# A hybrid decoder step on one core: attention steps nearer together, samples after the recurrence, pair closes later

## The chip, the cores and the metric

One core of a Trainium2 chip runs one launch of the program. The metric is the device time of the launch in microseconds (us); lower is better. The engines are TensorE (PE, matmuls and transposes), VectorE (DVE), ScalarE (ACT), GpSimd (POOL) and SyncE (SP), whose queue issues nearly all DMAs of this kernel. Each engine works through its own list of instructions in order, and semaphores hold an instruction back until what it needs is there.

## The reference, cut to what matters

One layer for a prompt of 1024 tokens and for 8 sample sequences with one new token each and caches of past keys and values; width 1024, 24 heads of 64 in three groups of 8.

```python
xn = rms_norm(x, norm_pre)
u, z_rnn, q, k, v, z_attn, g_rnn, g_attn = split(xn @ w_in)          # 1024 x 9216
uc, conv_new = causal_conv(u, conv_buf, conv_w, conv_b)
h, h_last = rg_lru(uc, h0, ...)        # r, i = sigmoid(block-diagonal products), a scan over tokens
y_rnn = (h * silu(z_rnn)) @ w_rnn_out
for g, (window, dilation) in enumerate(((128, 1), (512, 4), (2048, 16))):
    o, lse = dilated_attention(q[g], k[g], v[g], window, dilation, slopes[g])   # ALiBi, softmax
    # the prompt attends within itself; a sample token attends to 129 strided cache rows
y_attn = (merge_dilations(outs, lses) * silu(z_attn)) @ w_attn_out   # softmax over the three lse
mixed = sigmoid(g_rnn) * y_rnn + sigmoid(g_attn) * y_attn
out = x + rms_norm(mixed @ w_out, norm_post)
# also returned: the conv and recurrence states and the new k and v rows
```

## The kernel before

All products are in two-part form: an operand is a high and a low tile (`whi` and `wlo` for weights, written by ACT in line 274 and DVE in line 275), and a product is three matmuls, whi by x high, whi by x low, wlo by x high. Every matmul is recorded at line 183, every transpose by PE at line 187.

The work has these stages. First the norm and eight column blocks of `w_in`. Then the **pair phase**: 16 pairs of column blocks, each by seven products of combined operands (`project_pair`; the combined weights are the `wop` tiles, made by ACT in line 294 and DVE in lines 298 and 301). Products are added up in two tiles, `qa` and `qb` (DVE line 639, ACT line 641). When the fifth product is done, the closing operations of `qa` are put on a list to be emitted later (line 662), and after the seventh those of `qb` (line 666). What they are depends on the pair: a pair "a" takes a sigmoid on ACT (`zo`, line 847), multiplies on POOL (line 850) and stores to `zad` by DMA (line 673); a pair "v" copies to `vo` on ACT (line 829) and stores to `vd`. Beside the pairs runs the first half of the recurrence (`lru_front`, the tiles named `room`).

Then the **attention phase**: for each of four head pairs `hp` and three groups `g`, the projections of k and of q (192 projection matmuls for both, evicted into `kt` by DVE line 1026 and `qt` by ACT line 1022), and the attention of that group, in six steps (`attention`): scores into two PSUM banks, DVE adds the bias and takes the running extremes into `stat` (line 1135), ACT takes the exponential (line 1139), PE transposes `P` (line 1149, `turn`) and multiplies with `vn` (`values`). After a head pair's third group come `merge(hp)`, which weighs the three groups' outputs (`ot`; the weights go through DRAM, `fd` and `fb`), and the sample tokens' attention `sample(hp)`: a transpose of `qn`, a way through DRAM that spreads q over all partitions (`sd`, `qb`), keys from the cache (`ck`) multiplied on POOL and summed on DVE into `sc`, a transpose of `sc`, a softmax in `S`, a transpose of `S`, values from the cache (again `ck`) weighed on POOL (line 1372) and added on DVE (line 1375), and a sum by PE. Beside the first part of attention runs the second half of the recurrence (`lru_back`, lanes "lru" and "lru2", ACT lines 953 to 955 with a table load). Eight late gates follow (`proj_g`, evicted by ACT line 1427 into `sg`), and then the output products.

What sets the order: the program is written by one pass of the builder that keeps an emission clock, `clk`. Each projection matmul that is emitted moves the clock on. Work that is not on the main line stands in **lanes**, queues of generators; a generator yields the clock units after which it wants to be called again, and `tick` calls those that are due. `later` holds functions until the clock has reached their time, first in, first out. So a number such as `STEP` or 2500 is a distance in emitted matmuls, not a time, and the engines then run what stands in their queues as soon as their semaphores allow. Each lane runs one generator at a time: the samples stand in the lane "sample", one behind the other.

Most tiles come from an **arena** of 45 equal slots, whose free list is first in, first out (`Arena.get`). If none is free, the builder forces the clock on (`force`) until one is given back. The two lanes of the recurrence hold rooms of 4 slots each until they end (`lru_end`); a sample waits for 5 free slots (`SPARE`) before it loads. In attention there are three PSUM banks for scores and for all transposes of samples and merges (the tag "s"), used in turn. Before the seventh of the late gates the builder forces the clock until all four merges and samples are done:

```python
        if i == LATE_GATES - 2:
            until(lambda: len(merged) == 4 and len(sampled) == 4)
            spawn("split", split_ya())
```

Of the kernel before, what the change touches and what calls it, by code (L numbers as in the profile page):

```python
# [37 lines left out]

HALF = 520
OPS = 4  # L40
STEP = 3400
SPARE = 5
KY, VY = 3000, 4000
SLOPES = [[2.0 ** (-8.0 * (g * 8 + h + 1) / 24.0) for h in range(8)] for g in range(3)]
# [31 lines left out]
class Room:  # L76
# [15 lines left out]
    def close(self):  # L92
        self.arena.slots.extend(self.slots)
# [3 lines left out]
def hybrid_step(ctx: ExitStack, tc: tile.TileContext, I, O):  # L97
# [18 lines left out]
    def ps_tile(tag, n=1):  # L116
        own = MODES[mode[0]][tag]
        turns[tag] = i = turns.get(tag, -1) + 1
        b = own[i % len(own)]
        return banks[:, b] if n == 1 else banks[:, b:b + n]  # L120
# [4 lines left out]
    waiting, lanes, busy = [], {}, set()  # L125

    def later(delay, fn):
        waiting.append((clk[0] + delay, fn))

    def spawn(lane, gen, delay=0):  # L130
        lanes.setdefault(lane, deque()).append([clk[0] + delay, gen])
# [57 lines left out]
    def advance(gen):  # L189
        for _ in gen:  # L190
            tick()
# [326 lines left out]
    def mm3(out, wh, wl, mh, ml, first, last):  # L518
        mm(out, wh, mh, start=first, stop=False)
        mm(out, wh, ml, start=False, stop=False)  # L520
        mm(out, wl, mh, start=False, stop=last)
# [75 lines left out]
    def x21_back():  # L597
        while len(ar.slots) < 6:
            yield 500
        ts = [new([128, 2, HALF], F32, "xsum") for _ in range(2)]  # L600
        for q, t in enumerate(ts):
            nc.sync.dma_start(t, xd[2 * q:2 * q + 2].rearrange("k p c -> p k c"))
        yield 8000
        for k in range(4):
            x = new([128, 2, HALF], F32R, "x1b")
            src = ts[k // 2][:, k % 2]
            nc.scalar.activation(x[:, 0], src, AF.Copy)
            yield 700
            nc.vector.tensor_tensor(x[:, 1], src, f32(x[:, 0]), op=OP.subtract)
            X[1, k] = x  # L610
        ar.free(*ts)
# [3 lines left out]
    def x_op(name, k):  # L615
        if name[0] == "s":
            return SX[name, k]
        return X[int(name[1]) - 1, k + 4 * (int(name[2]) - 1)]

    def project_pair(close, last=False):  # L620

        i = W.use_pair()
        ta = new([128, 2, HALF], F32, "qa")
        quarter = lambda t, q: t[:, q].rearrange("p (c n) -> p c n", c=2)
        c11, c22 = quarter(ta, 0), quarter(ta, 1)
        for step, (wname, xname) in enumerate(STEPS):
            w = W.op(i, wname)
            if step == 1:
                tb = new([128, 2, HALF], F32, "qb")
                c21, c12 = quarter(tb, 0), quarter(tb, 1)  # L630
            p2 = ps_tile("c", 2)[:, :, :HALF // 2]
            for c in range(2):
                for k in range(4):
                    x = x_op(xname, k)[:, :, HALF // 2 * c:HALF // 2 * (c + 1)]
                    mm3(p2[:, c], w[:, 0, k], w[:, 1, k], x[:, 0], x[:, 1], k == 0, k == 3)
                    if k % 2:
                        W.work()
                        yield None
            add = lambda to, by: nc.vector.tensor_tensor(to, p2, by, op=OP.add)  # L639
            if step == 0:  # L640
                nc.scalar.activation(c11, p2, AF.Copy)
            elif step == 1:
                add(c12, c11)
            elif step == 2:
                add(c21, c12)
            elif step == 3:
                add(c12, c12)
                add(c22, c21)
            elif step == 4:
                add(c11, c11)  # L650
            elif step == 5:
                add(c21, c21)
            else:
                add(c12, c12)
            yield None
            W.drop(i, wname)
            if last and step == 3:
                for k in range(4):
                    ar.free(SX.pop(("s1", k)))
                spawn("sums", x21_back())  # L660
            if step == 4:
                later(2500, lambda: close(((0, 0, ta[:, 0]), (1, 1, ta[:, 1])), ta))
        W.pieces.pop(i)
        W.ops.pop(i)
        W.made.pop(i)
        later(2500, lambda: close(((0, 1, tb[:, 0]), (1, 0, tb[:, 1])), tb))

    def leave(dst, quarters, t, width=NT, then=None):

# [343 lines left out]
    def proj_qkv(g, hp, kind):  # L1013
        t = new([128, SEQ], F32, "qkv"[kind] + "t")
        (qts, kts)[kind][g, hp] = t

        def evac(c0, n, p):
            m = min(n, SEQ - c0)
            dst, src = grouped(t, g, c0, m), tokens(p, g, m)
            sd = smp[:, kind, 4 * g + hp]  # L1020
            if kind == 0:
                nc.scalar.activation(dst, src, AF.Copy, scale=C["qsc"][:, g, hp:hp + 1])
                if m < n:
                    nc.scalar.activation(sd, p[:, m:n], AF.Copy, scale=0.125)
            else:
                nc.vector.tensor_copy(dst, src)
                if m < n:
                    nc.vector.tensor_copy(sd, p[:, m:n])
        yield from project(evac)
# [22 lines left out]
    def load_v(g, hp):  # L1052
        t = vts[g, hp] = new([128, SEQ], F32, "vt")
        nc.sync.dma_start(t, vd[4 * g + hp])
# [49 lines left out]
    def attention(g, hp):  # L1104
# [80 lines left out]
        for i in range(6):  # L1185
# [12 lines left out]
            if i == 5:  # L1198
                ar.free(vns.pop((g, hp)))
                if g == 2:  # L1200
                    spawn("merge", merge(hp), 1000)
            yield STEP

# [322 lines left out]
    for q, (what, i) in enumerate(PAIRS):  # L1526
        advance(project_pair(pair_of(what, i), last=q == len(PAIRS) - 1))
        if q == 1:
            C = late_consts()
# [13 lines left out]

    room["P"] = new([128, 2, 2, 256], F32, "P")
    room["PT"] = [new([128, 2, 4, 128], F32, "PT") for _ in range(2)]
    for hp in range(4):
        for g in range(3):
            load_v(g, hp)
            for kind in (1, 0):
                advance(proj_qkv(g, hp, kind))  # L1550
            spawn("attention", attention(g, hp), 1000)
        spawn("sample", sample(hp), 1000)
# [203 lines left out]
```

## Time and profile before

| | us |
|---|---|
| median of 3 runs (lowest, highest) | 1280.31 (1277.37, 1282.57) |
| the profiled execution's own time | 1278.47 |
| its span | 1276.7 |
| PE busy in the span | 1221.2 (96%) |
| DVE, ACT, POOL busy | 756.2, 599.7, 261.6 |

The profile is of one execution. The busy times of the engines overlap; PE's share of the span says how little of it PE spends waiting. The granted clock that stands beside a stretch is TensorE's, as a share of full speed: 1.00 is 2.4 GHz throughout, and a stretch at less had a part at 1.2 GHz.

### The profile page before, as it was taken

To read this page: it belongs to the slowest core of one execution; us is meant where nothing else is said; L and a number is where in the kernel's file an instruction comes from. 1 tells how busy PE (TensorE), PEld (TensorE's weight loads), DVE (VectorE), ACT (ScalarE), POOL (GpSimd) and SP (SyncE) were. 2 spreads that over 40 slices of the span, in tenths; PEclk is the share of its full clock that TensorE was granted. 3 is DMA by queue.
4 is the path that set the end of the run, shared out by engine and by line. 5 is a ranking of instruction groups with operands and counts; after the bars stand their busy time and mean duration, and the time that the engine had idled before them with its cause. 6 is when DMAs were issued, how large, how long until landed. Compare 5 with 4: busy or idle time off the path is not lost. (4 is left out here: it accounts for less than half of the span.)

```text
span 1276.7 us, 24741 instructions
## 1 busy us (share of the span) xinstructions
PE 1221.2 (96%) x9949; PEld 1176.2 (92%) x9949; DVE 756.2 (59%) x1575; ACT 599.7 (47%) x1271; POOL 261.6 (20%) x280
## 2 busy tenths in 40 slices
PE   8999999999999978999799999899999979999997
PEld 8999999999999978899788989898999979999997
DVE  5558796777686653567477464555444545545226
ACT  7634445646545556756465343343568332222222
POOL 3011042102031201122224505310422210002001
PEclk9999999999999989999899999999999989999999
DMA  8053153436434294354653853651286466313105
GB/s 254 18 174 112 39 186 117 145 113 173 129 112 146 67 257 122 133 176 139 190 161 121 223 154 87 176 139 36 70 231 182 110 240 206 93 55 116 51 18 199
DMA packets 191161, 174.67 MB, mean 137 GB/s; under 512 B 55177, under 2 KB 162665, under 8 KB 191038
## 3 DMA queue, kind: packets, MB, share of 16 engines
q1 hardware_dynamic: 191046, 173.08, 44.5%
q8 instruction: 78, 1.28, 0.4%
q14 instruction: 37, 0.30, 0.1%
HBM read 122.67 MB, written 50.45 MB: 136 GB/s over the span
## 5 line engine op out<-in xcount | busy, mean ns | idle before, releaser
L183 PE MATMUL banks<-x,whi 128*128 128x256 f32 (+1 forms) x2048 | 386.5, 289 | 5.7 <-DVE qb L639 5.7
L183 PEld LDWEIGHTS banks<-x,whi 128*128 128x128 f32 x2048 | 320.1, 192 | 11.9 <-issue 10.6
L183 PE MATMUL banks<-x,wlo 128*128 128x256 f32 (+1 forms) x1024 | 290.6, 284 | 0.2 <-DVE wlo L334 0.2
L183 PE MATMUL banks<-s,wop 128*128 128x260 f32 x1536 | 197.7, 286 | 7.2 <-DVE wop L298 4.3
L183 PEld LDWEIGHTS banks<-s,wop 128*128 128x128 f32 x1536 | 192.1, 191 | 8.6 <-DVE wop L298 5.1
L183 PEld LDWEIGHTS banks<-x,wlo 128*128 128x128 f32 x1024 | 195.6, 191 | 0.4 <-DVE wlo L334 0.4
L275 DVE TENSOR_TENSOR wlo<-wraw,whi 128x512 fp32r<-128x512 f32 x112 | 93.6, 837 | 120.6 <-ACT whi L274 101.0
L183 PE MATMUL banks<-x,wop 128*128 128x260 f32 x1152 | 146.0, 282 | 0.3 <-DVE wop L298 0.2
L183 PEld LDWEIGHTS banks<-x,wop 128*128 128x128 f32 x1152 | 142.0, 188 | 0.7 <-DVE wop L298 0.7
L1139 ACT ACTIVATE P<-P,stat 128x128 f32<-128x128 f32 (+1 forms) x192 | 84.4, 441 | 70.3 <-DVE stat L1135 70.2
L183 PE MATMUL banks<-x1b,whi 128*128 128x264 f32 (+1 forms) x512 | 101.0, 294 | 16.4 <-ACT sg L1427 7.3
L183 PEld LDWEIGHTS banks<-x1b,whi 128*128 128x128 f32 x512 | 82.1, 196 | 18.8 <-ACT sg L1427 7.5
L183 PE MATMUL banks<-wlo,mh 128*128 128x256 f32 (+1 forms) x288 | 78.8, 280 | 0.0
L183 PE MATMUL banks<-x1b,wlo 128*128 128x256 f32 (+1 forms) x256 | 74.4, 290 | 0.0
L274 ACT ACTIVATE whi<-wraw 128x512 fp32r<-128x512 f32 x112 | 68.5, 621 | 12.4 <-DMA wraw<-in_w_in 10.8
L938 ACT ACTIVATE room<-banks,par 64x256 f32<-64x256 f32 (+2 forms) x96 | 52.2, 544 | 46.2 <-PE banks L183 45.0
L183 PE MATMUL banks<-whi,ml 128*128 128x256 f32 x256 | 71.9, 281 | 0.0
L183 PE MATMUL banks<-whi,mh 128*128 128x256 f32 x256 | 71.8, 280 | 0.0
L1135 DVE CUSTOM_DVE_ANT_0 P<-banks,base 128x128 f32<-128x128 f32 (+1 forms) x192 | 56.0, 348 | 17.4 <-PE banks L183 17.3
L294 ACT ACTIVATE wop<-wsum 128x512 fp32r<-128x512 f32 x48 | 30.1, 627 | 72.9 <-DVE wsum L301 59.3
L183 PE MATMUL banks<-hzh,wlo 128*128 128x256 f32 (+2 forms) x192 | 61.3, 319 | 0.0
L183 PE MATMUL banks<-hzl,whi 128*128 128x256 f32 (+2 forms) x192 | 61.3, 319 | 0.0
(280 smaller groups left out, 2270.5 us busy)
## 6 DMA issues: line engine op xcount, KB each, us to landing
wraw<-in_w_in SPq DMA_DIRECT2D x72, 512.0 KB
ck<-in_cache_kv_w SPq DMA_DIRECT2D x24, 512.0 KB
rxd<-room SPq DMA_DIRECT2D x16, 516.0 KB
room<-rxd SPq DMA_DIRECT2D x16, 516.0 KB
sgl<-sgd SPq DMA_DIRECT2D x16, 516.0 KB
xin<-in_x_prompt SPq DMA_DIRECT2D x16, 512.0 KB
vd<-vo SPq DMA_DIRECT2D x24, 256.0 KB
vt<-vd SPq DMA_DIRECT2D x12, 512.0 KB
```

The lines of the kernel that those rows point to most:

```text
L183: nc.tensor.matmul(out, lhsT, rhs, start=start, stop=stop)
L274: nc.scalar.activation(hi[:, a:b], raw[:, a:b], AF.Copy)
L275: nc.vector.tensor_tensor(lo[:, a:b], raw[:, a:b], f32(hi[:, a:b]), op=OP.subtract)
L294: nc.scalar.activation(w[:, 0], src, AF.Copy)
L938: nc.scalar.activation((a, t)[gate][rows, cs], p[at:at + 64, :n], AF.Sigmoid, bias=par[rows, b, 5 + gate:6 + gate])
L1135: nc.vector.tensor_tensor_reduce(out=pt[:, h, :128 * n], in0=ps[h][:, off:off + 128 * n], in1=base, scale=-SLOPES[g][2 * hp + h] * DIL[g], ...
L1139: nc.scalar.activation(pt[:, h, :128 * n], pt[:, h, :128 * n], AF.Exp, scale=-1.0, bias=st[:, g, 0, h, b:b + 1], accum_out=st[:, g, 1, h, ...
```

## The change

Three things change. `STEP`, the distance between two steps of an attention, is 2500 instead of 3400 clock units. The closing operations of a pair are emitted 4000 instead of 2500 units after their product. And a generator `lru_done` stands ahead of the first sample in the lane "sample": it ends when the lane "lru2" of the recurrence is empty, so that no sample is emitted until then. Lines from 1546 on are 5 higher in the changed kernel.

```diff
-STEP = 3400
+STEP = 2500
...
             if step == 4:
-                later(2500, lambda: close(((0, 0, ta[:, 0]), (1, 1, ta[:, 1])), ta))
+                later(4000, lambda: close(((0, 0, ta[:, 0]), (1, 1, ta[:, 1])), ta))
...
-        later(2500, lambda: close(((0, 1, tb[:, 0]), (1, 0, tb[:, 1])), tb))
+        later(4000, lambda: close(((0, 1, tb[:, 0]), (1, 0, tb[:, 1])), tb))
...
     room["PT"] = [new([128, 2, 4, 128], F32, "PT") for _ in range(2)]
+
+    def lru_done():
+        while "lru2" in lanes:
+            yield 1000
+    spawn("sample", lru_done())
     for hp in range(4):
```

The first place is ACT's queue at the close of the first pair "a", whose sigmoid is the row with `zo` (numbers behind a name are the builder's tile numbers). Before:

```order
L294 ACTIVATE wop_4210<-wraw_4045 128x512
L294 ACTIVATE wop_4228<-wsum_4212 128x512
L847 ACTIVATE zo_4238<-qa_4038 128x1040
L294 ACTIVATE wop_4256<-wraw_4045 128x512
L847 ACTIVATE zo_4312<-qb_4078 128x1040
L641 ACTIVATE qa_4281<-banks 128x520
L903 ACTIVATE lh<-lw 128x256
L907 ACTIVATE room_4244<-room_4243,par 128x1056
L294 ACTIVATE wop_4349<-wsum_4212 128x512
L294 ACTIVATE wop_4365<-wraw_4046 128x512
```

The same place now:

```order
L294 ACTIVATE wop_4210<-wraw_4045 128x512
L294 ACTIVATE wop_4228<-wsum_4212 128x512
L294 ACTIVATE wop_4254<-wraw_4045 128x512
L847 ACTIVATE zo_4264<-qa_4038 128x1040
L294 ACTIVATE wop_4286<-wsum_4212 128x512
L641 ACTIVATE qa_4279<-banks 128x520
L294 ACTIVATE wop_4317<-wraw_4046 128x512
L903 ACTIVATE lh<-lw 128x256
L907 ACTIVATE room_4242<-room_4241,par 128x1056
L847 ACTIVATE zo_4331<-qb_4076 128x1040
L294 ACTIVATE wop_4356<-wsum_4212 128x512
L294 ACTIVATE wop_4394<-wraw_4046 128x512
```

Three copies into `wop` (4254, 4286 and 4317) now stand ahead of the operations that they stood behind; before, the copies after `zo_4312` came behind lines 641, 903 and 907.

The second place is ACT's queue at the end of the pair phase, where the last pair "v" closes (`vo`) and the recurrence's first half ends (`room`, lines 907 and 922). Before:

```order
L907 ACTIVATE room_5314<-room_5313,par 128x1056
L274 ACTIVATE whi_5405<-wraw_5291 128x512 x2
L829 ACTIVATE vo_5478<-qa_5274 128x32x16 x2
L922 ACTIVATE room_5482<-room_5315 64x1032
L922 ACTIVATE room_5483<-room_5315 64x1032
L274 ACTIVATE whi_5524<-wraw_5522 128x512
```

Now:

```order
L907 ACTIVATE room_5310<-room_5309,par 128x1056
L294 ACTIVATE wop_5396<-wraw_5108 128x512
L274 ACTIVATE whi_5413<-wraw_5304 128x512 x2
L922 ACTIVATE room_5478<-room_5311 64x1032
L922 ACTIVATE room_5479<-room_5311 64x1032
L829 ACTIVATE vo_5499<-qa_5274 128x32x16 x2
L274 ACTIVATE whi_5524<-wraw_5522 128x512
```

The two copies into `vo` stand behind the recurrence's two operations instead of ahead of them.

The third place is PE's queue between the sixth and the seventh late gate, where the builder waits for all merges and samples (`mw` is merge 3's, `S`, `mn` and the matmuls from `one` are of sample 3, `smp` is for the sample rows). Before:

```order
L183 MATMUL banks<-x_7_32_132,whi_10711 128x264 x2
L183 MATMUL banks<-x_7_32_132,wlo_10712 128x264
L183 MATMUL banks<-one_2065,ck_10689 128x1 x8
L187 MATMUL banks<-ident,mw 48x128
L187 MATMUL banks<-ident,smp 96x128 x2
L183 MATMUL banks<-x_0_17_117,whi_10880 128x256 x2
```

Now:

```order
L183 MATMUL banks<-x_7_32_132,whi_10765 128x264 x2
L183 MATMUL banks<-x_7_32_132,wlo_10766 128x264
L187 MATMUL banks<-ident,S 128x64 x3
L183 MATMUL banks<-mn,e2n 128x24
L183 MATMUL banks<-one_2063,ck_10977 128x1 x8
L183 MATMUL banks<-x_0_17_117,whi_10892 128x256 x2
```

The last steps of sample 3 (`S`, `mn`, `one`) stand here directly one behind another, and merge 3's transpose (`mw`) stands earlier, among the gates.

## Rows read from the trace of the kernel before

**Rows 1.** Busy time of each engine, share of the span, instructions.

```profile
PE 1221.2 (96%) x9949; PEld 1176.2 (92%) x9949; DVE 756.2 (59%) x1575; ACT 599.7 (47%) x1271; POOL 261.6 (20%) x280
```

**Rows 2.** Stretches: length; busy us (instructions) by engine; granted clock; DMA share; GB/s.

```profile
460.00:500.00 40.00, 29.56 (x213) 28.79 (x213) 18.45 (x28) 23.11 (x32) 1.37 (x2) 0.88 0.60 148
500.00:605.00 105.00, 104.03 (x912) 95.75 (x913) 66.20 (x167) 67.60 (x157) 27.29 (x16) 1.00 0.49 153
605.00:690.00 85.00, 73.12 (x611) 66.31 (x609) 55.03 (x132) 47.02 (x104) 29.73 (x15) 0.94 0.55 167
690.00:1000.00 310.00, 304.08 (x2668) 281.40 (x2664) 163.91 (x481) 148.96 (x404) 89.92 (x41) 0.99 0.52 138
1000.00:1040.00 40.00, 32.74 (x251) 32.53 (x251) 16.22 (x27) 9.87 (x19) 15.13 (x6) 0.91 0.50 151
...
360.00:380.00 20.00, 18.07 (x138) 17.86 (x137) 19.41 (x24) 8.29 (x13) 2.43 (x1) 0.91 0.20 60
```

**Rows 3.** PE's waits by releaser: us in total, times, longest.

```profile
PE banks L187 <- DVE stat L1135: 8.3, 6, 3.7
PE banks L183 <- ACT sg L1427: 7.3, 1, 7.3
```

**Rows 4.** Timeline, first pair "a": start, us, instruction, [idle before <-releaser].

```profile
360.54 0.64 ACT L294 ACTIVATE wop<-wsum 128x512 fp32r<-128x512 f32 x1 [1.76 <-DMA zad<-qa]
...
363.77 4.44 PE L183 MATMUL banks<-s,wop 128*128 128x260 f32 x22 [1.93 <-DVE wop L298]
```

**Rows 5.** Timeline, end of the pair phase, ACT and PE.

```profile
465.53 2.01 ACT L829 ACTIVATE vo<-qa 128x512 f32<-128x512 f32 x2 [6.64 <-DVE qa L639]
...
472.41 0.77 PE L183 MATMUL banks<-x,whi 128*128 128x256 f32 x2 [5.65 <-DVE qb L639]
```

**Rows 6.** Timeline, recurrence beside attention and sample 0: ACT, DVE, PE.

```profile
613.30 1.28 ACT L955 ACT_TABLE_LOAD   x1
...
617.61 0.69 DVE L275 TENSOR_TENSOR wlo<-wraw,whi 128x512 fp32r<-128x512 f32 x1 [11.20 <-DMA out_kv_p<-kn]
...
618.85 0.80 PE L183 MATMUL banks<-x1b,whi 128*128 128x256 f32 x2 [5.85 <-DVE kt L1026]
```

**Rows 7.** Timeline, one calm attention step: PE, and ACT's last exponential.

```profile
924.45 0.82 PE L187 MATMUL banks<-ident,P 128*128 128x128 f32 x6
...
929.05 0.19 ACT L1139 ACTIVATION_READ_ACCUMULATOR P<-P,stat 128x1 f32 x1
...
930.79 0.82 PE L187 MATMUL banks<-ident,P 128*128 128x128 f32 x6
```

**Rows 8.** Timeline, sample 2 from the transpose of qn to that of sc.

```profile
806.37 0.27 PE L187 MATMUL banks<-ident,qn 128*24 128x128 f32 x1 [3.68 <-DVE stat L1135]
...
830.99 2.39 POOL L1324 TENSOR_TENSOR ck<-ck,qb 128x1024 f32<-128x1024 f32 x1 [5.03 <-DMA ck<-in_cache_kv_w]
...
846.20 0.52 PE L187 MATMUL banks<-ident,sc 128*64 128x128 f32 x3 [0.33 <-DVE stat L1135]
```

**Rows 9.** Chain that ended last, one piece of it; then the timeline at gate 7.

```profile
981.81 19.67 PE banks L183 x168
...
1027.58 1.06 ACT L1412 ACTIVATE yah<-ot 128x1024 fp32r<-128x1024 f32 x1 [10.84 <-POOL ot L1267]
...
1028.97 0.81 PE L183 MATMUL banks<-x1b,whi 128*128 128x264 f32 x2 [7.26 <-ACT sg L1427]
```

**Rows 10.** Timeline, sample 3 behind the transposes of S.

```profile
976.33 0.40 PE L187 MATMUL banks<-ident,S 64*128 64x64 f32 x3
...
978.00 6.19 POOL L1372 TENSOR_TENSOR ck<-ck,pT 128x1024 f32<-128x1024 f32 x3 [19.69 <-DMA out_kv_p<-kn]
...
990.27 1.22 DVE L1375 TENSOR_TENSOR ck<-ck,ck 128x1024 f32<-128x1024 f32 x1
```

**Rows 11.** Timeline, a sum on DVE beside a product on POOL.

```profile
420.72 2.78 DVE L301 TENSOR_TENSOR wsum<-wraw,wsum 128x512 f32<-128x512 f32 x1
...
420.52 2.43 POOL L850 TENSOR_TENSOR qa<-qa,zo 128x1040 f32<-128x1040 f32 x1 [20.95 <-ACT zo L847]
```

## The prediction

> **What bounds the kernel now.** I read the page's busy times first. TensorE (PE) is busy for 1221.2 us of the span of 1276.7 us, 96% [rows 1], and the chain that ended last runs through its matmuls, so a change gains only where PE stands still, or where its clock comes back sooner. Next I read the busy time by stretch [rows 2]: the reader is to subtract PE's busy time from the length of a stretch, and to look at the granted clock beside it. The end of the pair phase (460 to 500 us) idles 10.4 us at a mean clock of 0.88, the stretch in which the recurrence's second half runs beside attention and sample 0 (605 to 690) 11.9 us at 0.94, and the end of attention (1000 to 1040) 7.3 us at 0.91. Between them PE is nearly full: 1.0 us idle in 500 to 605, 5.9 us in 690 to 1000. Third I read what PE waited for [rows 3], and followed each long wait back in the timeline.
>
> A stall costs twice here. After the one of 5.65 us at 472.41 two matmuls take 0.77 us, where the 168 of the chain's long piece take 19.67 us, 0.117 each [rows 5, 9]: PE comes back at the lower of its two levels, 1.2 instead of 2.4 GHz. So a stretch's clock goes into the price.
>
> The terms below add up against the profiled execution, 1278.47 us; the median of the runs is 1280.31, 1.8 us above, and I add that at the end. From 0.5% on, some 6.4 us, a difference can be told from none.
>
> **Term 1: the closes of the pairs "a".** ACT copies a wop operand of the next product only after 1.76 us of waiting for the store of qa into zad, since the tile took the slot that qa gave back; 1.93 us of PE's time go [rows 4]. A second place, 66 us on, repeats it with 1.7 us. With closes 1500 clock units later the order has three of these copies ahead of the close, and they take other slots; qa's goes to a weight load, which is needed late. So both stalls go, 3.6 us. The slice of the first has clock 0.91 [rows 2], 1.8 us in 20, and the second's is the same: 3.6 us more. All of it would be -7.2; if the wait only moves, 0. I take -6.6, near the first end, since the row names its cause and the order removes that.
>
> **Term 2: the end of the pairs.** The last add into qb and with it the first product of attention is late by 5.65 us [rows 5]. Ahead of it on VectorE (DVE) stand the recurrence's products, which wait for ACT, and ACT first makes the two vo copies, 2.01 us for both [rows 5]. In the new order the vo copies stand behind the recurrence's two operations, so 2.0 us leave that chain, and one low-half split fewer stands ahead on DVE, 0.5. At best the whole 5.65 us goes, at worst nothing. I take -2.5.
>
> **Term 3: the recurrence without sample 0 beside it.** The samples' big tiles and the rooms of both recurrence lanes use up the arena here, so that tiles get slots whose old readers are still at work. DVE's wlo waited 11.20 us for the store of kn, and behind it on DVE stood the eviction of kt that PE needed: 5.85 us of stall [rows 6]. The stretch loses 11.9 us by idling and 0.06 of 85 us, 5.1, by its clock [rows 2], 17 in all. With the samples held back until lane "lru2" is empty, the pools force the clock on once instead of many times in this stretch, and the tile that waited for kn no longer does so there. The bounds are 0 (the wait finds another tile) and -17. I take -14, which leaves 3; the neighbouring stretch 500 to 605, with attention and recurrence but no shortage, keeps 1.0 us in 105.
>
> **Term 4: steps closer together.** A step was 36 projection matmuls after the last, and is now 24, so 12 x 0.117 = 1.4 us fewer stand between an exponential and the transposes that read it. The last exponential of a step ended at 929.24 and its transposes began at 930.79 [rows 7], 1.55 us of slack: 0.15 is left, enough for calm stretches. Beside the recurrence it isn't: its square root puts a table load of 1.28 us on ACT [rows 6], and eight blocks of that kind stand there. At worst each exposes 1.4 us, 11 in all; at best none does, since projections that the steps no longer interrupt follow undisturbed. I take +2, nearer to the 1.0 us of 500 to 605.
>
> **Term 5: four samples in less room.** They now start some 590 projection matmuls later. From the transposes of qn to those of sc, sample 2 took 806.37 to 846.20, 39.8 us; without the emission clock's pauses it would be 27.0 to the end of the third product on GpSimd (POOL) plus a reduction on DVE of some 1.2, by the add of equal size [rows 10], 28.2 us [rows 8]. The order now leaves PE work of about 33, 32, 38 and 28 us between the two. So the first three fit and the fourth just does. Another cost: a sample's or merge's transpose right behind scores takes a bank that DVE has yet to empty; before that cost 3.68 us at qn [rows 8], 8.3 us in six places [rows 3]. In the new order six such places stand 12 projection matmuls behind the scores or nearer. At 3.4 us each they'd cost 20; if the 1.4 us between cover the eviction, the stretch's 5.9 us of idling shrink by 4. I take +5.
>
> **Term 6: the tail.** Before, merge 3 ended last: its yah copy on ACT stood ahead of the gate's eviction, 7.26 us of stall [rows 9]. Now merge 3 is 350 projection matmuls earlier, and sample 3 ends last: S, e2n and samp_v stand directly one behind another on PE ahead of gate 6. From S to the third weighted product took 976.33 to 984.19, of which PE works 0.6; the add on DVE is 1.22 [rows 10]: 7.2 + 1.2 = 8.4 us of stall, 1.2 more than before. If sc or the V loads are late, up to 5 more. If other work of PE came to stand between them, the 7.26 would go without return. So -7 to +6; I take +3.
>
> A rule speaks against this change here. Beside POOL's 2.43 us product DVE's sum took 2.78 us [rows 11]; other sums of its form take 0.69. By the Trainium skill, SBUF — State Buffer, section "Who interferes with whom", a DVE instruction with two SBUF inputs and a GpSimd instruction that reads SBUF exclude each other, the second waiting the first out; the trace agrees. By that rule the first add of sample 3 would wait for the third product and the two adds would follow it, 1.2 us more in the tail: the sum would end 1.2 us higher.
>
> **Sum.** -6.6 - 2.5 - 14 + 2 + 5 + 3 = -13.1: 1278.47 becomes 1265.4, and with the 1.8 us of the median 1267.2.
>
> **Rivals.** *A: the collisions take the gain back.* If all six transposes behind scores cost the full 3.4 us, term 5 is 20 and the sum +2: 1282 on the median's scale, no difference that can be told. For it: PE's queue is in order, and a step now leaves 1.4 us less between scores and what follows. Against it: the collision at sc in a calm stretch was 0.33 us [rows 8], and only one of six reached 3.7 [rows 3].
>
> *B: the samples end too late, slower.* If the chain from qn to sc can't be had below the 39.8 us that sample 2 took [rows 8], since its loads queue behind stores on SP, the four gaps of 33, 32, 38 and 28 us miss it by 7, 8, 2 and 12, some 28 us in all, and PE stands still for them at sc. Term 5 is then 28 in place of 5, the sum +10, the time 1290. It decides from a chain of about 39 us; below 33 only sample 3 is hurt. For it: POOL's third product waited 5.03 us for its load [rows 8]. Against it: those loads went out late because the lane was paused.
>
> *C: the change doesn't remove the waits.* The arena is a first-in-first-out list, so another tile may get kn's or qa's slot, and an equal wait appears elsewhere. Half of terms 1 and 3 then: +10, 1277; with a quarter of it, 1272. For it: in the new order two small-store slots are still taken by wlo. Against it: the forced moments in the stretch fall to one.
>
> **How the numbers follow.** Forecast 0.55 (its own range 1254 to 1274), A 0.18, B 0.15, C 0.12. C's half and the forecast's low side count as faster: 0.55 + 0.06 + 0.03 of A = 0.64. Same: 0.06 of C, 0.12 of A, 0.03 of B = 0.21. Slower: 0.12 of B and 0.03 of A = 0.15. The range reaches from 1252 (terms 1, 3 and 6 at their lower ends, 13.6 lower, and a little of term 5) to 1286 (past A's 1282, short of B).
>
> **What would show it.** Term 1: no wait of PE for wop near 360 and 430 longer than 0.5 us. Term 2: PE's wait for qb falls to about 3 us. Term 3: no wait of DVE for kn's store, and clock 1.0 and under 4 us of idling in the recurrence's stretch. Term 4: PE waits for P behind ACT's table loads. Term 5: waits of PE for stat at sc, mw and qn. Term 6: one stall of some 8 us between gates 5 and 6, ended by ys or acc of sample 3 and not by ACT's sg. The forecast is wrong if PE waits for sc in three or more samples (B), or if idling in 605 to 690 stays above 8 us (C).

## The result, and the profile after

The changed kernel takes 1296.02 us (median of 4 runs, 1294.28 to 1297.21) where the kernel before takes 1278.99 (4 runs): ratio 1.0128, 95% interval 1.0101 to 1.0155. It is slower by 17 us where 13 us less were forecast. The profiled span is 1295.1 us, 18.4 us longer.

By stretch, with the columns of [rows 2]:

```profile
300.00:460.00 160.00, 156.61 (x1291) 156.05 (x1290) 122.25 (x163) 84.05 (x130) 37.68 (x42) 1.00 0.45 144
460.00:500.00 40.00, 32.91 (x244) 32.14 (x243) 16.01 (x24) 26.92 (x39) 2.24 (x2) 0.91 0.59 164
500.00:605.00 105.00, 100.53 (x852) 90.11 (x849) 63.06 (x168) 67.44 (x158) 21.78 (x13) 0.97 0.44 135
605.00:690.00 85.00, 84.38 (x736) 76.06 (x735) 52.80 (x150) 52.73 (x125) 16.82 (x10) 1.00 0.37 118
690.00:800.00 110.00, 95.80 (x794) 85.08 (x793) 63.21 (x173) 39.61 (x126) 47.36 (x22) 0.91 0.57 152
800.00:1000.00 200.00, 193.85 (x1680) 181.10 (x1679) 101.20 (x274) 87.76 (x234) 51.30 (x25) 0.99 0.54 152
1000.00:1060.00 60.00, 46.56 (x336) 45.88 (x337) 24.64 (x42) 15.21 (x26) 16.94 (x8) 0.86 0.36 120
```

Add to each stretch's idle time what its clock costs, the length times what the clock lacks of 1 (an estimate, since the column has two digits). Before, 460 to 500 lost 15.2 us, 500 to 605 1.0, 605 to 690 17.0, 690 to 1000 9.0, and 1000 to 1040 10.9, in all 53. After it is 10.7, 7.6, 0.6, 32.3 (24.1 of them in 690 to 800) and 21.8, in all 73. The stretch beside the recurrence has become whole, as forecast; the loss has come back right behind it and at the end, bigger. The loss grew by 20 us from 460 on; with 300 to 460, 6.8 us before and 3.4 now, by 16.5, and the span by 18.4.

PE's waits by releaser (total, times, longest):

```profile
PE banks L183 <- DVE ck L1375: 8.6, 1, 8.6
PE banks L183 <- ACT PT L1156: 6.6, 1, 6.6
PE banks L187 <- DVE stat L1135: 6.5, 2, 3.3
PE banks L187 <- DVE sc L1326: 6.4, 2, 4.0
PE banks L183 <- ACT smp L1024: 2.7, 1, 2.7
```

The waits for sg (7.3) and kt (5.9) are gone, and stat fell from 8.3 to 6.5 [rows 3, 6]. New are sc, ck and smp, and PT had 0.5. PT's wait, the longest inside attention, in the timeline (SP, then ACT, then PE):

```profile
696.49 3.09 SPq L1097 DMA_DIRECT2D out_kv_p<-kn  x4
699.68 0.80 SPq L1313 DMA_DIRECT2D qb<-sd  x1
...
702.85 3.06 SPq L259 DMA_DIRECT2D wraw<-in_w_in  x1
...
712.37 0.63 ACT L274 ACTIVATE whi<-wraw 128x512 fp32r<-128x512 f32 x1 [10.30 <-DMA wraw<-in_w_in]
...
713.32 0.70 PE L183 MATMUL banks<-PT,vn 128*64 128x128 f32 x4 [6.60 <-ACT PT L1156]
716.57 0.69 PE L183 MATMUL banks<-PT,vn 128*64 128x128 f32 x4 [2.55 <-DVE PT L1154]
```

PE names ACT's copy of PT, a 0.4 us operation. ACT's row says why it is late: the copy stands behind the split of the next weights, and ACT waited 10.3 us for them to land. They were issued at 702.85, behind the store of kn and four loads of sample 0, and needed at once. The second place is the end, where [rows 9] had one wait:

```profile
991.72 7.07 POOL L1262 TENSOR_TENSOR ot<-ot,fb 128x1024 f32<-128x1024 f32 x3
998.74 4.64 POOL L1324 TENSOR_TENSOR ck<-ck,qb 128x1024 f32<-128x1024 f32 x2
...
1002.39 0.30 PE L187 MATMUL banks<-ident,sc 128*64 128x128 f32 x1 [3.95 <-DVE sc L1326]
1005.11 0.42 PE L187 MATMUL banks<-ident,sc 128*64 128x128 f32 x1 [2.42 <-DVE sc L1326]
...
1020.14 4.25 DVE L1375 TENSOR_TENSOR ck<-ck,ck 128x1024 f32<-128x1024 f32 x2 [3.84 <-POOL ck L1372]
1024.44 1.86 PE L183 MATMUL banks<-one,ck 128*128 128x1 f32 x8 [8.63 <-DVE ck L1375]
```

Sample 3's second and third key products stand on POOL behind the three products of merge 3, sc waits for them, and the values' sum holds PE 8.63 us more. That is fifteen microseconds of waiting, at a clock of 0.86.

### The profile page after: what moved, and what is told of

It reads as the page before. It is cut to its first block, busy times and chain, and to the rows that moved or that the text cites. A ratio compares the mean times of both kernels' runs of the same rounds, so it can differ in the third digit from the quotient of the medians.

```text
span 1295.1 us, 24746 instructions
## 1 busy us (share of the span) xinstructions
PE 1230.9 (95%) x9949; PEld 1181.6 (91%) x9949; DVE 763.2 (59%) x1575; ACT 592.6 (46%) x1263; POOL 258.9 (20%) x280
## 5 line engine op out<-in xcount | busy, mean ns | idle before, releaser
L183 PE MATMUL banks<-x,whi 128*128 128x256 f32 (+1 forms) x2048 | 392.8, 292 | 4.4 <-DVE qb L639 3.9
L183 PE MATMUL banks<-s,wop 128*128 128x260 f32 x1536 | 194.9, 284 | 4.3 <-DVE qa L639 2.5
L275 DVE TENSOR_TENSOR wlo<-wraw,whi 128x512 fp32r<-128x512 f32 x112 | 90.0, 804 | 146.4 <-ACT whi L274 138.5
L183 PE MATMUL banks<-x1b,whi 128*128 128x264 f32 (+1 forms) x512 | 97.4, 287 | 3.2 <-ACT qt L1022 2.9
L274 ACT ACTIVATE whi<-wraw 128x512 fp32r<-128x512 f32 x112 | 69.5, 623 | 20.0 <-DMA wraw<-in_w_in 18.4
L298 DVE TENSOR_TENSOR wop<-wraw,wop 128x512 fp32r<-128x512 f32 x64 | 56.5, 883 | 13.8 <-ACT wop L294 13.7
L1022 ACT ACTIVATE qt<-banks,qsc 128x256 f32<-128x256 f32 x48 | 30.4, 640 | 68.2 <-PE banks L183 68.1
L183 PE MATMUL banks<-hzh,whi 128*128 128x256 f32 (+2 forms) x192 | 61.3, 319 | 0.0
```

Of the source, the lines that this page charges most:

```text
L183: nc.tensor.matmul(out, lhsT, rhs, start=start, stop=stop)
L274: nc.scalar.activation(hi[:, a:b], raw[:, a:b], AF.Copy)
L275: nc.vector.tensor_tensor(lo[:, a:b], raw[:, a:b], f32(hi[:, a:b]), op=OP.subtract)
L298: nc.vector.tensor_tensor(w[:, 1], src, f32(w[:, 0]), op=OP.subtract)
```

## The experiments

Theory L: the late samples cost, by sample 0's loads ahead of the weights and sample 3 at the end. Rival S: closer steps cost. First each part alone, and then the steps and the samples together (the lines of the diff above). All ratios are to the kernel before on the same chip.

**The three parts.** Steps alone:

```diff
-STEP = 3400
+STEP = 2500
```

> Only the distance of the attention steps is 2500; closes and samples as before. Theory L (the samples' late start is what costs: the weight load that is emitted behind sample 0's four loads, and sample 3 at the end of the gates): without the late start about as before, -4 to +4 us, no wait of ACT for a weight load over 6 us that holds PE, no sc wait at the tail. Rival S (steps closer together pack evictions, transposes and tiles too densely): +8 to +15 us against the kernel before, with PE's waits for PT, P and stat.

Measured 1297.4 us, ratio 1.0135 (1.0114 to 1.0157): the rival's size, and a little over. Its timeline (SP, ACT, PE):

```profile
694.99 3.71 SPq L1253 DMA_DIRECT2D fb<-fd  x6
...
699.37 0.43 SPq L259 DMA_DIRECT2D wraw<-in_w_in  x1
...
707.23 0.63 ACT L274 ACTIVATE whi<-wraw 128x512 fp32r<-128x512 f32 x1 [8.96 <-DMA wraw<-in_w_in]
708.50 0.80 PE L183 MATMUL banks<-x1b,whi 128*128 128x256 f32 x2 [6.10 <-ACT qt L1022]
...
751.88 0.63 ACT L274 ACTIVATE whi<-wraw 128x512 fp32r<-128x512 f32 x1 [11.99 <-DMA wraw<-in_w_in]
752.84 1.54 PE L183 MATMUL banks<-PT,vn 128*64 128x128 f32 x8 [7.85 <-ACT PT L1156]
```

Here it is a merge's six loads, and at the second place a sample's, that the weights stand behind. So the late weights need no late samples. The 17.5 us are a net figure: before's waits of PE for kt (5.85 us) and for sg (7.26 us) are gone in this run too, so the closer steps add more than that.

The samples' wait alone:

```diff
+    def lru_done():
+        while "lru2" in lanes:
+            yield 1000
+    spawn("sample", lru_done())
```

> Only the samples wait for the recurrence; steps 3400 and closes 2500 as before. Theory L: +15 to +25 us against the kernel before, with a tail in which PE waits for sc and for the values' sum of sample 3, 15 us in all. Rival S: within 5 us of before, since the recurrence's stretch loses its 17 us and the tail takes back some of it.

Measured 1295.76, ratio 1.0127 (1.0106 to 1.0148), as theory L had it, but in two halves. PE reaches sc of sample 3 at 984.3 us, with 3648 matmuls of x or x1b with whi or wlo behind it in the trace; before had the same count behind it at 999.6: 15 us gained, the size of the forecast's term 3. Then:

```profile
992.06 0.58 PE L187 MATMUL banks<-ident,S 64*128 64x64 f32 x3 [2.98 <-DVE S L1354]
...
999.47 1.93 POOL L1372 TENSOR_TENSOR ck<-ck,pT 128x1024 f32<-128x1024 f32 x1 [12.62 <-DMA ck<-in_cache_kv_w]
1001.36 6.93 POOL L1262 TENSOR_TENSOR ot<-ot,fb 128x1024 f32<-128x1024 f32 x3
1008.25 1.93 POOL L1372 TENSOR_TENSOR ck<-ck,pT 128x1024 f32<-128x1024 f32 x1
...
1010.21 3.35 DVE L1375 TENSOR_TENSOR ck<-ck,ck 128x1024 f32<-128x1024 f32 x1 [16.73 <-POOL ck L1372]
...
1021.07 1.23 PE L183 MATMUL banks<-one,ck 128*128 128x1 f32 x5 [28.07 <-DVE ck L1375]
```

Sample 3's values are loaded when they are needed, and its products share POOL with merge 3, which with the old steps is late too. That makes 28 us in one wait, 34 with the three ahead of it.

The closes alone:

```diff
-                later(2500, lambda: close(((0, 0, ta[:, 0]), (1, 1, ta[:, 1])), ta))
+                later(4000, lambda: close(((0, 0, ta[:, 0]), (1, 1, ta[:, 1])), ta))
...
-        later(2500, lambda: close(((0, 1, tb[:, 0]), (1, 0, tb[:, 1])), tb))
+        later(4000, lambda: close(((0, 1, tb[:, 0]), (1, 0, tb[:, 1])), tb))
```

> Only the closes of the pairs are emitted 4000 later. Both theories: the time at which attention's projections begin (third of them, after the qt wait) moves from 496 to about 490 us, as in the changed kernel, and the whole run by the same -6 us. Rival: tile slots change hands in attention too, and the run moves by more than 5 us away from that.

Measured 1274.69, ratio 0.9953 (0.9936 to 0.997), -5.2 us; the third of attention's projections begins at 490.4 us where it was 496.3. As expected.

Steps and samples without the closes:

> Steps 2500 and samples after the recurrence, closes as before. Theory L: the changed kernel without its early gain, +23 us against the kernel before (17 + 6). If the closes' 6 us are lost again behind a later wait, it is +17, the same as the changed kernel.

Measured 1303.53, ratio 1.017 (1.0143 to 1.0198), +23.6 us, and the whole change has +17: the closes' gain is kept. But +17.5 and +15.9 for the parts add up to 33.4, not 23.6. The trace shows one reason: closer steps bring merge 3 forward, and PE's waits for sc and the sum at sample 3's end are 14.1 us here in place of the 31.4 with the late samples alone.

**The late weights.** In the changed kernel a sample loads the next weights ahead of its keys:

```diff
+            W.load(W.pos + 2, SPARE)
             kq[g] = load_k(g)
```

> The changed kernel, but a sample loads the next weights ahead of its own keys: at 703 us one weight load moves ahead of four of sample 0's loads on SP's queue, and PE's order stays the same. Theory W (the wait of 10.3 us of ACT for the weights, and so PE's waits of 6.6 and 2.6 us and the half clock behind them, come from the place of that load in the queue): the weights are issued 3 us earlier and land some 6 us earlier, both waits of PE fall to 3 us in all, and the run is 8 to 12 us faster than the changed kernel, about 1285. Rival (the steps' 1.4 us less of slack in itself holds PE): the waits stay, within 3 us of the changed kernel.

Measured 1294.02, ratio 1.0118 (1.0103 to 1.0133): 2 us under the changed kernel, and not the gain of theory W. The first wait went all the same, 6.60 us of PE's wait became 0.60, while the one behind it stayed (2.55 us, now 2.81). Most of what was gained went at the next weights:

```profile
706.23 0.63 ACT L274 ACTIVATE whi<-wraw 128x512 fp32r<-128x512 f32 x1 [4.31 <-DMA wraw<-in_w_in]
...
729.91 0.63 ACT L274 ACTIVATE whi<-wraw 128x512 fp32r<-128x512 f32 x1 [8.51 <-DMA wraw<-in_w_in]
...
730.57 2.84 DVE L275 TENSOR_TENSOR wlo<-wraw,whi 128x512 fp32r<-128x512 f32 x1 [11.53 <-ACT whi L274]
...
734.23 1.02 PE L187 MATMUL banks<-ident,cst 128*20 128x128 f32 x4 [7.73 <-DVE stat L1135]
```

Read from below: PE waits for DVE's stat, DVE was held by the split of the weights' low half, that by ACT's, that by the load, which stands behind merge 0's store and loads. So a merge's loads were given the same rule:

```diff
         while len(ar.slots) < 8:
             yield 500
+        W.load(W.pos + 2, 5)
```

> The changed kernel with the next weights loaded ahead of a sample's keys and ahead of a merge's weights. The run with the first alone took PE's wait of 6.6 us away, and the wait for stat at the recurrence's transpose rose from 3.2 to 7.7 us, behind the next weight load, which stands behind merge 0's store and six loads on SP. Theory W: with that load ahead of merge 0 too, that wait falls below 3.5 us and the run is 5 to 10 us faster than the changed kernel, 1286 to 1291. Rival: the wait moves on to the next late tile, within 3 us of the changed kernel (1294).

Measured 1293.25, ratio 1.0107 (1.0088 to 1.0127), 2.8 us under the changed kernel: the rival's size. The wait at 734 is 4.0 us (for vn now) instead of 7.7, and where the rest went was not found in one place. With the steps alone the same two edits do more:

> Steps 2500 alone, with the weights loaded first in both places. In the run with the steps alone ACT waited 8.96 and 11.99 us for weights and PE 6.1 and 7.9 us; here both loads stand ahead of the merge's and the sample's. Theory W: both waits of PE fall below 2 us, and the run is 12 to 18 us faster than with the steps alone, 1280 to 1285. Rival (what closer steps cost stands in many short waits at the transposes of P and in the products with PT): at most 8 us faster, 1289 or more.

Measured 1282.16, ratio 1.0023 (1.0008 to 1.0038): 15 of the steps' 17.5 us go, and the waits of 6.10 and 7.85 us are gone. There the late weights are most of the net cost. In the whole change they are a small part, 2.8 us here and 9 once the tail is shortened (below). The kernel before was not run with the weights first and its old steps; with steps of 3400 in another setting the same edits gain 2 to 4 us (the last run below), which suggests that most of the 15 belongs to the closer steps.

**The tail.** The changed kernel with shorter pauses in the sample lane:

```diff
-KY, VY = 3000, 4000
+KY, VY = 2000, 2500
```

> The changed kernel with the sample lane's pauses KY 2000 and VY 2500 in place of 3000 and 4000: sample 3's sc stands 144, its S 72 projection matmuls ahead of gate 6's end. Theory T (the tail stall is sample 3 being emitted without a gap): the waits for sc (6.4 us) and most of the 8.6 us for the sum of the values go, and 5 us of half clock: 10 to 14 us faster than the changed kernel, about 1284. Rival: the tail's waits only change their names (loads of the values are late), within 4 us.

Measured 1288.87, ratio 1.0077 (1.0058 to 1.0096), 7 us under the changed kernel, between the two forecasts. The 8.6 us for the sum went to 0.35. But sc still waits 4.3 and 3.9 us, and not behind merge 3: its products begin on POOL at 991.86, behind all three of sample 3's key products, and these waited for their loads from the cache (the first 39.9, the second 2.2 us). So merge 3 on POOL is not the only thing that makes sc late.

The same pauses with steps of 3400, closes 4000 and late samples:

> Steps 3400 as before, closes 4000, samples after the recurrence, and the sample lane's pauses 2000 and 2500. If the late samples gain 15 us in the recurrence's stretch, as the run with them alone did until its tail, and sample 3 now ends ahead of gate 6: merge 3 is still the last and costs the 7 us of before, so 1280 - 5 - 15 = 1260. If sample 3's loads still meet merge 3's at the end: 1270 or more.

Measured 1247.72 us, ratio 0.9754 (0.9741 to 0.9766): 31 us faster than before, 12 more than expected. Nearly all the waits of attention have gone:

```profile
500.00:980.00 480.00, 473.50 (x4168) 435.95 (x4167) 285.28 (x783) 261.39 (x662) 144.10 (x71) 1.00 0.53 153
980.00:1040.00 60.00, 58.60 (x420) 58.40 (x420) 41.51 (x48) 20.92 (x32) 17.09 (x6) 1.00 0.67 232
```

6.5 us idle in 480, at a clock of 1.00, and 1.4 in the tail's 60. Against it, the steps of the last head pair alone at 2500:

```diff
-            yield STEP
+            yield 2500 if hp == 3 else STEP
```

> As the run before, and the steps of the last head pair alone 2500 apart, so that merge 3 ends ahead of gate 6 too. Theory: the last stall, 7 us and 4 us of clock behind it, goes as well: 1249 to 1254. Rival: closer steps cost in themselves, wherever they stand (half clock in the last quarter of attention): 1260 or more.

Measured 1252.9, ratio 0.9796 (0.9784 to 0.9809). The time lies in the theory's range, but that range was counted from 1260; from 1247.7 it is 5 us slower where a gain of 7 and more was meant, so neither forecast holds. The last stall was already down to 1.4 us, so there was little to gain, and the closer steps cost 5 us in a quarter of attention, in four waits of 1.0 to 2.2 us and what the clock adds to them.

What the samples' wait is worth without a tail, by leaving it out:

> Closes 4000 and the short pauses, steps 3400, samples not held back: against the fastest run so far (1247.7) it lacks only the samples' wait for the recurrence. If that wait is worth the 14 us of term 3 of the forecast, 1260 to 1266, with DVE's wait for the store of kn and PE's for kt still there; if the short pauses make up the gain, 1248 to 1253.

Measured 1269.6, ratio 0.9921 (0.9899 to 0.9943). That is slower than either range. DVE's wait for the store of kn (11.1 us) and PE's for kt (5.7) are there, as expected without the samples' wait. So the wait for the recurrence is worth 22 us (21 when each run is taken against before on its own chip), more than term 3's 14, and the short pauses by themselves 5 (1274.7 to 1269.6).

**What closer steps still cost.** The changed kernel with the short pauses and the weights first:

> The changed kernel with the short pauses in the sample lane and the weights first in both places; the same with steps 3400 and without the latter took 1247.7. If the late weights make up most of the 41 us between 1288.9 and 1247.7, it is 1270 or less; if closer steps cost in themselves, 1278 to 1287.

Measured 1279.8, ratio 0.9997 (0.998 to 1.0014). Weights make 9 of the 41 us between 1288.9 and 1247.7; 32 stay.

```profile
500.00:980.00 480.00, 464.39 (x3975) 422.79 (x3971) 280.46 (x760) 243.31 (x633) 129.56 (x66) 0.98 0.50 143
980.00:1040.00 60.00, 50.81 (x387) 49.75 (x388) 27.84 (x42) 18.33 (x34) 25.68 (x11) 0.89 0.40 134
```

The first row has 15.6 us idle and 9.6 by the clock, the second 9.2 and 6.6, against 6.5 and 1.4: 33 us. So 14 of the 33 stand in the tail, which is sc of sample 3 once more, waiting for key products that wait for their loads; merge 3 comes behind them:

```profile
980.03 2.35 POOL L1326 TENSOR_TENSOR ck<-ck,qb 128x1024 f32<-128x1024 f32 x1 [2.68 <-DMA ck<-in_cache_kv_w]
983.69 0.42 PE L187 MATMUL banks<-ident,sc 128*64 128x128 f32 x1 [4.68 <-DVE sc L1328]
986.39 7.46 POOL L1263 TENSOR_TENSOR ot<-ot,fb 128x1024 f32<-128x1024 f32 x3
```

The rest stands in a few places between 539 and 844 us, of different kinds, each with a stretch of lower clock: first scores (below), PT at 710, P at 784 (1.78 us), merge 2's transpose at 843.

```profile
537.49 1.06 ACT L955 ACTIVATE room<-room 128x1032 f32<-128x1032 f32 x1
538.46 0.68 ACT L1022 ACTIVATE qt<-banks,qsc 128x256 f32<-128x256 f32 x1
...
539.19 1.23 PE L183 MATMUL banks<-kt,qt 64*128 64x256 f32 x4 [2.72 <-ACT smp L1024]
...
710.49 0.70 PE L183 MATMUL banks<-PT,vn 128*64 128x128 f32 x4 [2.81 <-DVE PT L1154]
...
843.43 0.41 PE L187 MATMUL banks<-ident,mw 128*48 128x128 f32 x1 [3.27 <-DVE stat L1135]
```

With steps of 2500 a group ends before the next begins, so its first scores follow 12 projection matmuls behind the projection, and need a qt that ACT evicts behind the recurrence's functions. Of first scores this is the only long wait. Is it this early start that costs, or the density?

```diff
-            spawn("attention", attention(g, hp), 1000)
+            spawn("attention", attention(g, hp), 4000)
```

> As the run with short pauses and the weights first (steps 2500, samples late, closes 4000; 1279.8), but each group's attention begins 4000 in place of 1000 clock units behind its projection. If the early first scores cost: PE's wait of 2.7 us at 539 us for ACT's eviction goes, and with it the half clock at five such places, and the run falls by 15 us or more, to 1265 or less. If the dense steps cost in themselves: within 6 us of 1279.8.

Measured 1280.68, ratio 1.0006 (0.9991 to 1.0021). The number is the one forecast for the density, but it can't be read so, since one long wait of its own appeared.

```profile
673.46 0.69 DVE L1065 COPY vn<-banks 128x512 f32<-128x512 f32 x1 [9.51 <-POOL room L972]
...
674.21 1.11 PE L187 MATMUL banks<-ident,vt 128*128 128x128 f32 x4 [18.79 <-DVE vn L1065]
```

DVE's copy into vn waited for the recurrence's product on POOL (line 972), which stood behind merge 0's three products. That vn had got a slot which this product still read is the likely reason, not shown. In 640 to 690 us this run idles 22.9 us at a clock of 0.73, some 36 us lost; in the rest of 500 to 1040 it loses 13, and nothing in the tail, where the run with the early start loses 41 in all. That speaks for the early start, but the run doesn't decide it. The other run, between the two distances:

```diff
-STEP = 2500
+STEP = 2900
```

> As the run with short pauses and the weights first, with steps 2900 in place of 2500 (30 projection matmuls), and groups still beginning 1000 units behind their projection. If the early first scores cost, the lane is as empty as with 2500 (6 x 2900 is less than the 20000 units of a group's projections) and most of the 32 us stays: 1270 or more. If the density of the steps costs, about half goes: 1262 to 1266 or less.

Measured 1262.56, ratio 0.9859 (0.9841 to 0.9876). Half of the cost goes with 400 of the 900 units. That is the time forecast for the density, but this run doesn't decide either, since the lane, expected to be empty at 2900, is not. Counted in projection matmuls of the trace from the start of the kernel (x or x1b with whi or wlo), the scores of the second to the fourth group begin at 1164, 1356 and 1548 with steps of 2500, 12 behind the end of their projection. With 2900 they begin at 1200, 1428 and 1644, nearly as with 3400 (1200, 1428, 1656). So the early start has gone here too, and with it the wait at 539.

Last, the weights first with steps of 3400:

> Steps 3400, closes 4000, samples late, short pauses (1247.7), and the weights first in both places. With steps 3400 no wait of PE behind a weight load is left in that run's trace, so nothing is to be had: within 3 us of 1247.7 by either theory; a gain above 4 us would say that weights are late there too.

Measured 1245.49 us, ratio 0.9721 (0.9704 to 0.9739), the fastest kernel of the study, 34 us under before and 50 under the change. It is 2 us under the same without it, 3.4 when each is taken against before on its own chip: at the edge of what was expected. With the rest alike, steps of 2500, 2900 and 3400 take 1279.8, 1262.6 and 1245.5. That closer steps cost is shown; whether by their density or by the early start of the groups stays open.

## Why the prediction was wrong

The sign was wrong, and the time lies 10 us above the range. The step that failed is **term 4**, with **term 6** beside it. Terms 1 to 3 had the right mechanism, 1 and 2 at two thirds of their size.

Terms 1 and 2, forecast -9.1: -6.4 at 490 us, and -5.2 in a run of their own. At 363 and 430 us no wait for wop is left, but of the 3.6 us two small ones are new, 0.91 us for wop at 324 and 0.77 for qa at 373. PE's last wait for qa ends 4.4 us earlier than before (459.27 for 463.64), where term 1 had 6.6. At the end of the pairs the rows of [rows 5] now read:

```profile
461.17 2.15 ACT L922 ACTIVATE room<-room 64x1032 fp32r<-64x1032 f32 x2 [6.13 <-DVE room L913]
463.35 1.98 ACT L829 ACTIVATE vo<-qa 128x512 f32<-128x512 f32 x2
...
466.25 0.48 PE L183 MATMUL banks<-x,whi 128*128 128x256 f32 x2 [3.87 <-DVE qb L639]
```

vo stands behind the recurrence's two operations, and the wait is 3.87 us, 1.8 less, where 2.5 was taken.

Term 3, forecast -14: right. 605 to 690 lost 17.0 us and loses 0.6, and DVE's wait for the store of kn is gone; alone the edit is 15 us ahead until the tail, and with the tail mended it is worth 22.

Term 4, forecast +2 with 11 as the worst: +17.5 alone. The step priced one thing, the slack between an exponential and its transposes, by a calm stretch [rows 7], and there it was right: PE's waits for P come to 1.6 us in five places, the longest 0.5. It left out what else closer steps move: merges, their loads and their slots come earlier, while the recurrence still holds its rooms. The load of the next weights then goes out behind those loads, late (that it had no slot before is read from the builder's code, not shown). No term of the sum had a late load of attention's weights in it, though ACT's split stands in the queue ahead of PT and qt. The prediction followed the moved steps along PE's queue and not along SP's. With the weights first, 15 of the 17.5 us went, shown. In the whole change closer steps cost 34 us even with the weights first and the short pauses, shown by the runs at 2500 and 3400. Where these stand is read in the trace, some 14 us in sample 3's tail and the rest in a few places between 539 and 844 us; whether the density or the early start of each group makes them stays open.

Term 5, forecast +5: the waits for stat behind scores were two of 3.3 us (cst and mw), not six, 6.5 us where before had 8.3; PE did not wait for sc in samples 0 to 2. So this part of the term cost nothing, and rival A fell. What did not hold is that sample 3's chain just fits in 28 us: from qn at 969.5 PE reached sc 28.7 us later, and the last transpose of sc began 35.6 us later. This cost stands under term 6.

Term 6, forecast +3 with 6 as the worst: the tail lost 21.8 us where it lost 10.9. The 8.4 us worked out for the values' sum was 8.63, by luck: the three weighted products ended 6.8 us behind S, not 7.9, and two adds followed the third product where the term had one. DVE's first add began at 1020.14, beside that product, and ended at 1023.07, 1.1 us behind it, as the prediction's sentence on VectorE and GpSimd has it. The 5 us allowed for a late sc were 6.4, and a clock of 0.86 in 1000 to 1060 us came on top. The sum had taken merge 3 for done because its transposes stood earlier on PE, and did not look at its products, which stand between sample 3's on POOL; the run with short pauses shows that sample 3's loads are late besides.

Rival B named the right sign and 1290, in part by luck: of its four gaps only sample 3's was missed, by 6.4 us, where its price had all four. Rival C did not happen; the waits removed did not come back under their names. None of the signs that the prediction gave for being wrong came either, since none looked at the loads of the weights.

## What to carry to other kernels

When a change emits one kind of work earlier, list the loads that it moves ahead of others, and look for the load whose use is nearest: when it goes out late, the queue in front of it becomes a stall on engines that have no part in the change. A run that is to separate two causes should be looked at in its queue order first: here the distance of 2900 took away the early start as well. A part that gains in its own stretch and loses at the end should be judged with the end mended: the samples' wait was +16 us by itself, and -22 with short pauses, late closes and the old steps. And a stage that ends "earlier on PE" has ended only when the last engine in its chain has, here GpSimd.

## What the runs showed of the hardware

The split of the weights' low half on DVE, 0.69 us by itself [rows 6], took 2.84 us beside a product on POOL (730.57, above), and an add of the values 3.35 us in place of 1.22 (1010.21, [rows 10]). The products on POOL:

```profile
730.52 2.34 POOL L1264 TENSOR_TENSOR ot<-ot,ot 128x1024 f32<-128x1024 f32 x1
...
1010.14 2.34 POOL L1264 TENSOR_TENSOR ot<-ot,ot 128x1024 f32<-128x1024 f32 x1
```

Both DVE operations begin while the product runs and end behind it, 0.55 and 1.08 us later; both read two tiles in SBUF, as the sum in [rows 11] does. PE's clock makes short waits dear: in 690 to 800 us 14.2 us of waiting went with a mean clock of 0.91, another 9.9 us.
